# A new instruction order in the first pass and the first attention pairs of a two-layer decoder trunk

## The chip, the core and the metric

The kernel runs on one core of a Trainium2 chip, in one launch. The metric is device time in microseconds (us) of that launch. The kernel before took 774.13 us, the median of three runs (773.55 to 778.01).

## What is computed

The reference is a decoder trunk of two layers over 256 tokens of width 1024, all float32. A conditioning vector c gives each layer six modulation vectors by one large product, `silu(c) @ w_ada`. Each layer has a token mixer and a gated convolutional feed-forward block, each ahead of it normalised and modulated:

```python
for i in range(2):
    mod = jax.nn.silu(c) @ w_ada[i] + b_ada[i]
    sh1, sc1, g1, sh2, sc2, g2 = jnp.split(mod, 6, axis=-1)
    h = rmsnorm(x, norm_mix[i]) * (1 + sc1) + sh1
    y = dilated_mixture(h, ...) if i == 0 else gla_mixer(h, ...)
    x = x + g1 * y
    h = rmsnorm(x, norm_ffn[i]) * (1 + sc2) + sh2
    x = x + g2 * conv_ffn(h, ...)
return rmsnorm(x, norm_final)
```

The mixer of layer 0, the one that the change touches, has 16 heads of width 64 in three dilation groups. It needs `h @ w_in` for query, key and value of each group and head, scores with a relative bias, a softmax and the product with the values.

## The kernel before

**Arithmetic.** Activations lie transposed: 8 tiles `h[kt]` of 128 features by 256 tokens. A float32 product is made of three single-pass products: each weight tile and each activation tile is split into a rounded high part and a low part (the rest), and `mm3` (L172) issues high by high (L175), weights high by activation low (L176) and weights low by activation high (L177) into one PSUM bank. `split` (L155) loads a weight tile from memory into a buffer `raw`, ScalarE rounds it (`whi`, L165), VectorE subtracts (`wlo`, L169). There are four `raw` buffers, which the modulation weights share, and three each of `whi` and `wlo`. A buffer is handed on when its last reader is done.

**Queues.** All weight loads are issued in order by one queue, that of SyncE. Each compute engine executes its own instructions in order too. A planner that works with estimated durations orders the instructions of each engine at compile time; `with behind(i)` and `issue_after(i)` force what stands inside to come after instruction i on i's engine. PSUM has eight banks: two with the tag p, four with s, two with t. A new tile takes a bank of its tag when the tile that held it has been read for the last time.

**Start.** TensorE spreads c over the partitions (tile `cb`, L123), ScalarE applies silu (L124) into `c_bc`. The squares of x are summed (L357 to L363), TensorE adds them over the partitions (`ms`, L187), and ScalarE makes the reciprocal root (L189, L191). `keep_warm` (L266) issues matmuls whose result nobody reads. Three small matmuls (L377) make the bias rows in PSUM banks with tags t, t and s, and ScalarE copies them out (L392).

**First pass (L381 to L394 and L563 to L572).** For each of the 8 feature tiles VectorE makes two dot products of modulation weights with `c_bc` (`ada_chunk`, L138), ScalarE adds the offsets (L146, L148), VectorE scales x (`xr`, L257), ScalarE shifts and rounds (`hhi`, L259), VectorE takes the rest (`hlo`, L260) and the low part of 1920 columns of weights in two halves of 960. With these TensorE makes the projections of heads pair 0 and pair 1: twelve query and key products of 256 columns and two value products of 384, three matmuls each. The banks are s, s, s, p, p for pair 0 and its values and s, t, t for pair 1.

**Pairs 1 to 7.** `values` makes the value projections from two loads of 768 KB, `queries` a group's query and key from one of 1 MB, `evacuate` copies them from PSUM, `scores` makes the scores, `probabilities` the softmax, `turn` transposes the probabilities on TensorE through banks with the tag t (the copies out of it alternate between ScalarE and VectorE, L464), and `outputs` (L467) multiplies by the values. After each `queries` follows a chunk of modulation weights (`next_ada`). `load_bias` (L337) issues eight small loads per pair. After the first pass come, in this order, the first half of pair 1's values, the scores of pair 0, the second half, the first group of pair 2, the scores of pair 1, and then a loop over pairs 2 to 7 (L600 to L628).

Of the kernel before, what the change touches and what calls it, by code (L numbers as in the profile page):

```python
# [18 lines left out]
P = 128  # L19
D = 1024  # L20
# [37 lines left out]
def trunk(ctx: ExitStack, tc: tile.TileContext, I, out):  # L58
# [59 lines left out]


    c_bc = const.tile([P, D], F32, name="c_bc")  # L120
    for n in range(2):
        ps = bank("cb", "t")
        last_c = mm(ps, ones_d[:1, :], c_row[:1, 512 * n : 512 * n + 512], start=True, stop=True)  # L123
        silu = nc.scalar.activation(c_bc[:, 512 * n : 512 * n + 512], ps, AF.Silu, scale=float(D))  # L124


    mod = {}

    def ada_chunk(l, n, dmas=1):
# [4 lines left out]
        for s in range(2):  # L134
            piece, kt = ADA_ORDER[2 * n + s]
            dot = tmp.tile([P, 1], F32, tag="dot", name="dot", bufs=4)
            w = raw[:, D * s : D * s + D]
            nc.vector.tensor_tensor_reduce(  # L138
                w, w, c_bc, op0=ALU.mult, op1=ALU.add, scale=1.0, scalar=0.0, accum_out=dot,
            )  # L140
# [103 lines left out]

    @contextmanager
    def behind(*those):

        with ExitStack() as st:
            for i in those:
                st.enter_context(tc.issue_after(i.ins))  # L250
            yield

    def normed(l, sub, r, kt):
# [10 lines left out]
        return h_hi[kt], h_lo[kt]  # L264

    def keep_warm(n):  # L266

        ps = bank("warm")
        for i in range(n):
            mm(ps[:, :P], ones_d, ones_d, start=True, stop=True)  # L270

# [78 lines left out]

    sq = wspl.tile([P, 2048], F32, tag="wlo", name="sq").rearrange("p (k t) -> p k t", k=KT)
    with behind(last_c):
        keep_warm(4)
    nc.vector.tensor_tensor(sq[:, 0:4, :], x_all[:, 0:4, :], x_all[:, 0:4, :], op=ALU.mult)  # L357
    with behind(silu):
        for i in (4, 6):
            last_sq = nc.scalar.activation(sq[:, i : i + 2, :], x_all[:, i : i + 2, :], AF.Square)  # L360
    for n in (0, 4):
        for m in (2, 1):
            last_add = nc.vector.tensor_tensor(sq[:, n : n + m, :], sq[:, n : n + m, :], sq[:, n + m : n + 2 * m, :], op=ALU.add)  # L363
        if n == 0:
            with behind(last_add):
                last_add = scale_terms(0)
    exp_ln_after(last_sq)
# [11 lines left out]
    first = norm_ops[1], last_add  # L379
    w0, h = [], []  # L380
    for kt in range(KT):  # L381
        with behind(*first):
            term = ada_chunk(0, kt, dmas=1 if kt else 2)
        h.append(normed(0, 0, r, kt))
        if kt:
            w0.append(split(I["w0"][kt], 15 * P))
        else:
            with behind(chain[0][1]):
                w0.append(split(I["w0"][kt], 15 * P, 2, after=((term,), (chain[0][0],))))
            with behind(copied[0]):  # L390
                for ps, c in rows_ps:
                    nc.scalar.copy(rows[:, c], ps)  # L392
            first = (last_lo[0],)
        if kt == 1:  # L394
            scale_terms(1)
    with tc.issue_after(last_load[0].ins):
# [30 lines left out]

    def probabilities(s, bias):


        m = tmp.tile([P, 16], F32, tag="m", name="m")
        normed_p = []
        prob = [att.tile([P, KEYS + 2], F32, tag="prob", name="prob", bufs=6) for _ in range(4)]
        for i in range(4):
# [5 lines left out]
                op0=ALU.add, op1=ALU.max, scale=1.0, scalar=-3e38, accum_out=m[:, i : i + 1],  # L440
            )
        for h in range(2):
            rs, n = slice(2 * h, 2 * h + 2), KEYS + 2 * h
# [41 lines left out]

    last_q = [None]

    def evacuate(q, k, g, pq, pk):

        if g:
            last_q[0] = nc.scalar.mul(q[g], pq, 0.125)
            return nc.vector.tensor_copy(k[g], pk)
        qh, ql = q[0]
        nc.scalar.mul(qh, pq, 0.125)
        nc.vector.scalar_tensor_tensor(ql, pq, 0.125, qh.bitcast(F32), op0=ALU.mult, op1=ALU.subtract)
        pk = in_order(pk)
        kh, kl = (as_tokens(z[:, 0:T]) for z in k[0])
        nc.scalar.copy(kh, pk)  # L500
        return nc.vector.tensor_tensor(kl, pk, kh.bitcast(F32), op=ALU.subtract)

# [19 lines left out]

    def values(u, half, pv):
        with behind(*chain[7]):
            w = split(I["wv"][u - 1, half], 1536)
        for k4 in range(4):
# [6 lines left out]

    def queries(u, g, q, k, tag="p", after=()):
        w = split(I["wqk"][u - 2, g], 2048, after=(after, after))
        pqk = bank("pqk", tag)
        pq, pk = pqk[:, :T], pqk[:, T:]
        for kt in range(KT):
# [5 lines left out]
        with behind(evacuate(q, k, g, pq, pk)):  # L544
            next_ada()
        return middle, end

# [9 lines left out]

    b0 = [bank("pqk", tg) for tg in "ssspp"]
    pqk0 = [b[:, T * i : T * i + T] for b in b0[:3] for i in range(2)]
    pv = b0[3:]  # L560
    b1 = [bank("pqk", tg) for tg in "stt"]
    pqk1 = [b[:, T * i : T * i + T] for b in b1 for i in range(2)]
    for kt in range(KT):  # L563
        s, e = kt == 0, kt == KT - 1
        for i in range(2 * NG):
            mm3(pqk0[i], parts(w0[kt], P * i), h[kt], s and i % 2 == 0, e and i % 2 == 1)
        wv = parts(w0[kt], 6 * P, NG * P)
        for t in range(2):
            ht = [y[:, P * t : P * t + P] for y in h[kt]]
            mm3(pv[t][:, : NG * P], ht, wv, s, e)  # L570
        for i in range(2 * NG):
            mm3(pqk1[i], parts(w0[kt], 9 * P + P * i), h[kt], s and i % 2 == 0, e and i % 2 == 1)  # L572

    qk0, qk1 = new_qk(), new_qk()
    v = by_groups(pv)
    for qk, pqk, g in ((qk0, pqk0, 0), (qk1, pqk1, 0), (qk0, pqk0, 1), (qk0, pqk0, 2), (qk1, pqk1, 1), (qk1, pqk1, 2)):
        evacuate(*qk, g, pqk[2 * g], pqk[2 * g + 1])
    pv = [bank("pv", "p") for _ in range(2)]
    end = values(1, 0, pv)
    bias = bias_of(0)  # L580
    with behind(end):
        s, last = scores(*qk0)
    with behind(last):
        values(1, 1, pv)
    v0, v = v, by_groups(pv)
    before = probabilities(s, bias)

    qk = new_qk()
    with behind(last):
        end = queries(2, 0, *qk, tag="t", after=last_q)  # L590
    bias = bias_of(1)
    with behind(end[1]):
        turn((0, 1), *before)
        s, last = scores(*qk1)
    with behind(last):
        turn((2, 3), *before)
        outputs(0, v0, before[1])
    before = probabilities(s, bias)

    for u in range(2, NPAIR):  # L600
        if u > 2:
            bias = bias_of(u)
            qk = new_qk()
            with behind(last):
                queries(u, 0, *qk)
        middle, end = queries(u, 1, *qk)
        if u == 2:
# [5 lines left out]
        with behind(end):  # L613
            turned = turn((2, 3), *before)
        queries(u, 2, *qk)
        pv = [bank("pv", "p") for _ in range(2)]
        end = values(u, 0, pv)
        if u < NPAIR - 1:
            end = values(u, 1, pv)
# [7 lines left out]
        v = by_groups(pv)  # L627
        before = probabilities(s, bias)  # L628

# [543 lines left out]
```

## Time and profile before

| | |
|---|---|
| runs | 773.55, 774.13, 778.01 us; median 774.13 us |
| the profiled execution | 777.02 us, of which 775.1 us from the first to the last instruction (the span) |
| TensorE (PE) busy | 755.9 us, 98% of the span |
| VectorE (DVE) busy | 633.7 us, 82% |
| ScalarE (ACT) busy | 484.7 us, 63% |
| mean granted TensorE clock | 0.994 |
| DMA | 186.29 MB, mean 240 GB/s |

A busy TensorE is not one at its peak, since the ends of matmuls are modelled; the distance from one matmul's start to the next says more. Idle time of TensorE and stretches at a lower granted clock are what a new order could remove. The first 60 us are the start and the first pass, the stretch from there to about 275 us the attention pairs, and then come the output projection and the second half of layer 0, and layer 1.

### The profile page before, as it was taken

The page shows a single profiled execution, that of the slowest core. Times are in us where ns is not written, and L with a number is a line of the kernel's source. Part 1 is how long each engine was busy: PE and PEld are TensorE (multiplying, and loading weights), DVE is VectorE, ACT ScalarE, POOL GpSimd, SP SyncE. Part 2 cuts the span into 40 slices and gives each one's busy share as a digit, 9 for nine tenths or more (in the row PEclk, how much of TensorE's full clock was granted, in tenths as well). Part 3 has the DMA queues.
Part 4 walks back from the last instruction along what each step waited for, and adds up shares of the span by engine and source line. Part 5 has one row for each costly group of instructions (what it writes and reads, how often), then busy time and mean ns, then how long its engine had stood idle before and what let it go on. Part 6 is the DMA issues. An engine that isn't in the chain of part 4 may idle for free.

```text
span 775.1 us, 15908 instructions
## 1 busy us (share of the span) xinstructions
PE 755.9 (98%) x6416; PEld 731.5 (94%) x6416; DVE 633.7 (82%) x1136; ACT 484.7 (63%) x948; POOL 12.4 (2%) x36
## 2 busy tenths in 40 slices
PE   8899899999999999999999999999999999999997
PEld 5899899999999999999999998898999999999997
DVE  6996787779879968999998877797667998899662
ACT  5566564655666668766666556746667776667552
POOL 0000000000000010000000100000010000000000
PEclk9999999999999999999999999999999999999999
DMA  8988687686887847767646985966245665555741
GB/s 344 413 296 315 186 315 242 231 327 198 319 313 257 296 163 261 272 224 270 209 160 213 353 297 180 344 243 235 95 166 188 219 218 187 194 199 205 252 161 55
DMA packets 36199, 186.29 MB, mean 240 GB/s; under 512 B 8412, under 2 KB 10972, under 8 KB 19870
## 3 DMA queue, kind: packets, MB, share of 16 engines
q1 hardware_dynamic: 35744, 184.84, 66.8%
q8 instruction: 50, 0.82, 0.4%
q10 hardware_dynamic: 382, 0.45, 0.2%
q14 instruction: 23, 0.19, 0.1%
HBM read 184.17 MB, written 1.10 MB: 239 GB/s over the span
## 4 chain that ended last, share of the span: by engine, by line
PE 71%; DMA 12%; DVE 11%; ACT 3%; issue 1%; SPq 0%; DVEq 0%; ACTq 0%
PE pab L176 10%; PE pab L175 10%; PE pab L177 10%; DMA raw<-in_wqk 8%; DVE wlo L169 5%; PE pd L175 5%; PE pd L177 5%; PE pd L176 5%; DMA raw<-in_wv 3%; PE pqk L175 3%; PE pqk L176 2%; DVE ada_raw L138 2%; PE pqk L177 2%; PE py L175 2%; PE py L176 2%; PE py L177 2%
## 5 line engine op out<-in xcount | busy, mean ns | idle before, releaser
L169 DVE TENSOR_TENSOR wlo<-raw,whi 128x1024 fp32r<-128x1024 f32 (+3 forms) x274 | 291.8, 1098 | 62.8 <-ACT whi L165 62.1
L165 ACT CAST whi<-raw 128x1024 fp32r<-128x1024 f32 (+3 forms) x274 | 245.8, 945 | 131.9 <-PE pab L176 41.3
L177 PE MATMUL pab<-hhi,wlo 128*128 128x256 f32 x672 | 184.9, 276 | 0.0
L176 PE MATMUL pab<-hlo,whi 128*128 128x256 f32 x672 | 184.8, 277 | 0.0
L175 PE MATMUL pab<-hhi,whi 128*128 128x256 f32 x672 | 183.4, 277 | 0.0
L176 PEld LDWEIGHTS pab<-hlo,whi 128*128 128x128 f32 x672 | 126.1, 188 | 0.2
L177 PEld LDWEIGHTS pab<-hhi,wlo 128*128 128x128 f32 x672 | 126.2, 188 | 0.0
L175 PEld LDWEIGHTS pab<-hhi,whi 128*128 128x128 f32 x672 | 125.2, 188 | 0.1
L175 PE MATMUL pqk<-hhi,whi 128*128 128x256 f32 x440 | 120.8, 286 | 2.6 <-ACT hhi L259 2.6
L177 PE MATMUL pqk<-hhi,wlo 128*128 128x256 f32 x440 | 121.7, 281 | 0.0
L176 PE MATMUL pqk<-hlo,whi 128*128 128x256 f32 x440 | 121.6, 280 | 0.0
L138 DVE CUSTOM_DVE_ANT_0 ada_raw<-ada_raw,c_bc 128x1024 f32<-128x1024 f32 x96 | 113.6, 1222 | 6.6 <-DMA ada_raw<-in_w_ada 6.6
L177 PE MATMUL pd<-ghi,wlo 128*128 128x256 f32 x352 | 97.1, 276 | 0.0
L176 PE MATMUL pd<-glo,whi 128*128 128x256 f32 x352 | 97.1, 276 | 0.0
L175 PE MATMUL pd<-ghi,whi 128*128 128x256 f32 x352 | 96.8, 276 | 0.0
L175 PEld LDWEIGHTS pqk<-hhi,whi 128*128 128x128 f32 x440 | 82.3, 191 | 3.8 <-ACT hhi L259 3.1
L177 PEld LDWEIGHTS pqk<-hhi,wlo 128*128 128x128 f32 x440 | 83.4, 190 | 0.3 <-issue 0.3
L176 PEld LDWEIGHTS pqk<-hlo,whi 128*128 128x128 f32 x440 | 83.5, 190 | 0.1
L176 PEld LDWEIGHTS pd<-glo,whi 128*128 128x128 f32 x352 | 66.1, 188 | 0.0
L177 PEld LDWEIGHTS pd<-ghi,wlo 128*128 128x128 f32 x352 | 66.1, 188 | 0.0
L175 PEld LDWEIGHTS pd<-ghi,whi 128*128 128x128 f32 x352 | 65.9, 188 | 0.0
L734 ACT ACTIVATE r<-pab,small 128x256 f32<-128x256 f32 x86 | 46.6, 558 | 15.6 <-DVE r L737 15.5
(210 smaller groups left out, 1266.4 us busy)
## 6 DMA issues: line engine op xcount, KB each, us to landing
ada_raw<-in_w_ada SPq DMA_DIRECT2D x47, 1024.0 KB, 5.8
raw<-in_w_up SPq DMA_DIRECT2D x42, 1024.0 KB, 4.9
raw<-in_w_down SPq DMA_DIRECT2D x32, 704.0 KB, 5.1
raw<-in_wqk SPq DMA_DIRECT2D x18, 1024.0 KB, 6.6
raw<-in_wv SPq DMA_DIRECT2D x14, 768.0 KB, 4.6
raw<-in_w SPq DMA_DIRECT2D x7, 960.0 KB, 6.5
raw<-in_w_out_a SPq DMA_DIRECT2D x4, 1024.0 KB, 7.2
raw<-in_w_v_b SPq DMA_DIRECT2D x4, 1024.0 KB, 6.4
```

Source lines behind the costliest of these rows:

```text
L138: nc.vector.tensor_tensor_reduce(w, w, c_bc, op0=ALU.mult, op1=ALU.add, scale=1.0, scalar=0.0, accum_out=dot,)
L165: copied[0] = nc.scalar.copy(hi[:, c], raw[:, c])
L169: last_lo[0] = nc.vector.tensor_tensor(lo[:, c], raw[:, c], hi[:, c].bitcast(F32), op=ALU.subtract)
L175: mm(ps, a[0], b[0], start=start, stop=False)
L176: mm(ps, a[0], b[1], start=False, stop=False)
L177: return mm(ps, a[1], b[0], start=False, stop=stop)
L734: nc.scalar.activation(r, u[:, :T], AF.Identity, scale=cw[2], bias=col(C_CB + 44 * l + f))
```

## The change

- **Start.** Four `keep_warm` matmuls go to the head of TensorE's queue, ahead of the spreading of c. The two Squares on ScalarE go between the two silus. The second `keep_warm`, five matmuls, comes behind the bias rows, and the projections come behind it.
- **First pass on VectorE and ScalarE.** The order is written out by hand. Per tile: the two dot products, the first part of the low weights of the tile before (768 columns), `xr`, the second part (1152 columns), `hlo`; on ScalarE the offsets, `hhi`, and then both parts of `whi`. Tiles 0 and 1 have an order of their own. The copies of the bias rows come behind the `hhi` of tile 1.
- **First pass on TensorE.** The three products go by parts: high by high for a whole tile, then activation low, then weights low, the last of these interleaved with the next tile's. The banks are s, t, t, p, p and s, s, s.
- **Behind the pass.** Pair 2's first group comes first, by parts, then the scores of pair 0, both halves of pair 1's values, the scores of pair 1. The softmax is cut into `maxima` and `probabilities`. The outputs of pair 0 and the transposes of pair 1 move into the loop's turn for pair 2.
- **Transposes.** They use two t and two s banks, and ScalarE makes all copies.

```diff
+    keep_warm(4)
     c_bc = const.tile([P, D], F32, name="c_bc")
 ...
+        with behind(*((last_sq,) if n else ())):
+            silu = nc.scalar.activation(c_bc[:, 512 * n : 512 * n + 512], ps, AF.Silu, scale=float(D))
+        if n == 0:
+            with behind(silu):
+                for i in (4, 6):
+                    last_sq = nc.scalar.activation(sq[:, i : i + 2, :], x_all[:, i : i + 2, :], AF.Square)
 ...
     with behind(norm_ops[0]):
-        keep_warm(3)
 ...
-            mm(ps, tab[:, 16 * g : 16 * g + 16], oh[:33, c], start=True, stop=True)
+            last_row = mm(ps, tab[:, 16 * g : 16 * g + 16], oh[:33, c], start=True, stop=True)
             at += n
+    with behind(last_row):
+        warm = keep_warm(5)
 ...
+    dots(0)
+    scaled(0)
+    cast(0, 0)
+    shifted(0)
+    cast(0, 1)
+    rest_of(0)
+    low(0, 0)
+    dots(1)
+    low(0, 1)
+    scaled(1)
+    shifted(1)
+    rest_of(1)
+    with behind(on_act[0]):
+        for ps, c in rows_ps:
+            on_act[0] = nc.scalar.copy(rows[:, c], ps)
+    for kt in range(2, KT):
+        for half in range(2):
+            cast(kt - 1, half)
+        dots(kt)
+        low(kt - 1, 0)
+        scaled(kt)
+        low(kt - 1, 1)
+        shifted(kt)
+        rest_of(kt)
 ...
-            t = bank("t", "t")
+            t = bank("t", "ttss"[i])
 ...
-            (nc.vector.tensor_copy if i % 2 else nc.scalar.copy)(pt[:, i, :], t[:, 0:KEYS])
+            nc.scalar.copy(pt[:, i, :], t[:, 0:KEYS])
 ...
-    b0 = [bank("pqk", tg) for tg in "ssspp"]
+    b0 = [bank("pqk", tg) for tg in "sttpp"]
 ...
-    b1 = [bank("pqk", tg) for tg in "stt"]
+    b1 = [bank("pqk", tg) for tg in "sss"]
+    last = [warm]
+    def products(kt, part, pieces):
+        w, y = w0[kt][part == 2], h[kt][part == 1]
+        with behind(*last):
 ...
+        last[0] = i
     for kt in range(KT):
 ...
+        if kt:
+            products(kt - 1, 2, (0,))
+        products(kt, 0, range(3))
+        if kt:
+            products(kt - 1, 2, (1, 2))
+        products(kt, 1, range(3))
+    products(KT - 1, 2, (0,))
+    products(KT - 1, 2, (1, 2))
 ...
+    pq, pk, middle, end = raw_queries(2, 0, tag="t", low=left[2][1:], by_parts=True)
 ...
     with behind(end):
         s, last = scores(*qk0)
 ...
     with behind(last):
+        values(1, 0, pv, low=left[-1][1:])
+    end = values(1, 1, pv, after=left[-1][:1], low=evacuated[1:])
 ...
+    with behind(end):
         s, last = scores(*qk1)
+    raised = maxima(s, bias1)
 ...
+        if u == 2:
+            turned_pt, before = before[1], probabilities(*raised)
+        middle, end = queries(u, 2, *qk)
+        if u == 2:
+            with behind(end):
+                outputs(0, v0, turned_pt)
+                turn((0, 1), *before)
```

In the helpers `dots`, `scaled`, `shifted`, `rest_of`, `cast` and `low` each instruction stands behind the one that the order names before it on its engine (`on_dve`, `on_act`). `cast` and `low` work on columns 0 to 767 (the projections of pair 0) and 768 to 1919. The loads of tiles 0 and 1 go in two pieces.

## Rows read from the trace of the kernel before

**Rows 1.** The page's first section: busy time, share of the span, instructions of each engine.
```profile
PE 755.9 (98%) x6416; PEld 731.5 (94%) x6416; DVE 633.7 (82%) x1136; ACT 484.7 (63%) x948; POOL 12.4 (2%) x36
```

**Rows 2.** TensorE's waits, whole span: waiter, releaser, us in total, times, longest.
```profile
PE t L463 <- ACT pt L464: 4.3, 4, 2.6
...
PE pqk L175 <- ACT hhi L259: 2.6, 2, 2.2
...
PE po L471 <- DVE pt L464: 0.9, 1, 0.9
PE pv L175 <- DVE k L494: 0.8, 1, 0.8
PE s L418 <- DVE k L501: 0.8, 1, 0.8
```

**Rows 3.** Timeline of TensorE: start, duration, instruction, count, [idle before, releaser].
```profile
6.74 2.07 PE L270 MATMUL warm<-ones_d 128*128 128x128 f32 x8
...
11.87 1.47 PE L377 MATMUL rows<-oh,tab 33*16 33x512 f32 x6
13.72 0.62 PE L175 MATMUL pqk<-hhi,whi 128*128 128x256 f32 x3 [0.38 <-ACT hhi L259]
...
21.74 1.01 PE L175 MATMUL pqk<-hhi,whi 128*128 128x256 f32 x3 [2.25 <-ACT hhi L259]
...
28.63 0.52 PE L175 MATMUL pqk<-hhi,whi 128*128 128x256 f32 x3
...
33.84 0.52 PE L175 MATMUL pqk<-hhi,whi 128*128 128x256 f32 x3
...
59.87 0.34 PE L175 MATMUL pv<-whi,hhi 128*128 128x384 f32 x1
```

**Rows 4.** Two stretches of 3 us: busy per engine (instructions), granted clock, DMA share, GB/s.
```profile
22.00:25.00 3.00, 3.00 (x13) 3.00 (x14) 3.00 (x7) 2.32 (x4) 0.00 (x0) 0.50 1.02 417
83.50:86.50 3.00, 3.00 (x15) 3.00 (x16) 3.00 (x11) 0.37 (x1) 0.00 (x0) 0.50 0.96 401
```

**Rows 5.** Timeline of VectorE in the first pass.
```profile
9.58 1.22 DVE L138 CUSTOM_DVE_ANT_0 ada_raw<-ada_raw,c_bc 128x1024 f32<-128x1024 f32 x1
...
12.41 0.48 DVE L257 SCALAR_TENSOR_TENSOR xr<-x_all,mod,rstd 128x256 f32<-128x256 f32 x1 [0.46 <-ACT mod L146]
...
16.24 1.22 DVE L138 CUSTOM_DVE_ANT_0 ada_raw<-ada_raw,c_bc 128x1024 f32<-128x1024 f32 x1
...
18.53 2.22 DVE L169 TENSOR_TENSOR wlo<-raw,whi 128x960 fp32r<-128x960 f32 x2
...
23.35 0.48 DVE L260 SCALAR_TENSOR_TENSOR hlo<-xr,mod,hhi 128x256 fp32r<-128x256 f32 x1
...
28.57 0.48 DVE L260 SCALAR_TENSOR_TENSOR hlo<-xr,mod,hhi 128x256 fp32r<-128x256 f32 x1
```

**Rows 6.** Timeline of ScalarE in the first pass.
```profile
6.84 0.60 ACT L124 ACTIVATE c_bc<-cb 128x512 f32<-128x512 f32 x1 [1.11 <-PE cb L123]
7.34 1.14 ACT L360 ACTIVATE sq<-x_all 128x512 f32<-128x512 f32 x2
...
13.16 0.50 ACT L259 ACTIVATE hhi<-xr,mod 128x256 fp32r<-128x256 f32 x1
...
14.45 0.88 ACT L392 COPY rows<-rows 16x512 f32<-16x512 f32 x3
...
49.18 1.90 ACT L165 CAST whi<-raw 128x960 fp32r<-128x960 f32 x2 [0.45 <-DMA raw<-in_w]
```

**Rows 7.** The copies of the bias rows (L392): who waited for them (us, times).
```profile
  PEld pqk L175: 0.2, 1
```

**Rows 8.** Timeline of ScalarE around 82 us.
```profile
80.62 1.99 ACT L165 CAST whi<-raw 128x1024 fp32r<-128x1024 f32 x2 [3.11 <-DMA raw<-in_wqk]
...
82.92 0.47 ACT L464 COPY pt<-t 128x384 f32<-128x384 f32 x1
```

**Rows 9.** Timeline of TensorE: the transposes at 83 us.
```profile
83.45 0.90 PE L463 MATMUL t<-ident,pn 128*128 128x128 f32 x3 [2.65 <-ACT pt L464]
```

**Rows 10.** The chain that ended last: start us, us, what.
```profile
66.86 13.68 DMA raw<-in_wqk
...
251.20 0.45 PE pv L175
```

More of the change, by code (lines that the diff above doesn't have):

```diff
@@ L117, in scale_terms, with behind, keep_warm @@
                                               op0=ALU.add, op1=ALU.mult)
+    @contextmanager
+    def behind(*those):
+        with ExitStack() as st:
+            for i in those:
+                st.enter_context(tc.issue_after(i.ins))
+            yield
+    def keep_warm(n):
+        ps = bank("warm")
+        for i in range(n):
+            i = mm(ps[:, :P], ones_d, ones_d, start=True, stop=True)
+        return i
+    keep_warm(4)
     c_bc = const.tile([P, D], F32, name="c_bc")
+    sq = wspl.tile([P, 2048], F32, tag="wlo", name="sq").rearrange("p (k t) -> p k t", k=KT)
     for n in range(2):
@@ L123, in trunk @@
         last_c = mm(ps, ones_d[:1, :], c_row[:1, 512 * n : 512 * n + 512], start=True, stop=True)
-        silu = nc.scalar.activation(c_bc[:, 512 * n : 512 * n + 512], ps, AF.Silu, scale=float(D))
-    mod = {}
+        with behind(*((last_sq,) if n else ())):
[4 more added lines that the diff above has]
+                    last_sq = nc.scalar.activation(sq[:, i : i + 2, :], x_all[:, i : i + 2, :], AF.Square)
+    mod, last_dot = {}, [None]
     def ada_chunk(l, n, dmas=1):
@@ L243, in trunk @@
     squared = [None, None]
[L245 to L251, printed above, removed]
     def normed(l, sub, r, kt):
@@ L264, in normed @@
         return h_hi[kt], h_lo[kt]
[L266 to L270, printed above, removed]
     early_x = [state.tile([P, T + 16], F32, tag=f"ex{k}", name="early_x") for k in range(KT)]
@@ L351, in load_bias @@
         return both
-    sq = wspl.tile([P, 2048], F32, tag="wlo", name="sq").rearrange("p (k t) -> p k t", k=KT)
-    with behind(last_c):
-        keep_warm(4)
     nc.vector.tensor_tensor(sq[:, 0:4, :], x_all[:, 0:4, :], x_all[:, 0:4, :], op=ALU.mult)
-    with behind(silu):
-        for i in (4, 6):
-            last_sq = nc.scalar.activation(sq[:, i : i + 2, :], x_all[:, i : i + 2, :], AF.Square)
     for n in (0, 4):
@@ L363, in trunk @@
             last_add = nc.vector.tensor_tensor(sq[:, n : n + m, :], sq[:, n : n + m, :], sq[:, n + m : n + 2 * m, :], op=ALU.add)
[L364 to L367, printed above, removed]
+    with behind(last_add):
+        on_dve = [scale_terms(0)]
+    exp_ln_after(silu)
     r = rstd_of([sq[:, 0, :], sq[:, 4, :]])
@@ L376, in trunk @@
             rows_ps.append((ps, c))
-            mm(ps, tab[:, 16 * g : 16 * g + 16], oh[:33, c], start=True, stop=True)
+            last_row = mm(ps, tab[:, 16 * g : 16 * g + 16], oh[:33, c], start=True, stop=True)
             at += n
[L379 to L395, printed above, removed]
+    with behind(last_row):
+        warm = keep_warm(5)
@@ new lines, in trunk, with dots @@
+    w0, h, xr, raw0 = [], [], [None] * KT, []
+    pieces = (slice(0, 6 * P), slice(6 * P, 15 * P))
+    on_act = [norm_ops[1]]
+    def dots(kt):
+        with behind(on_dve[0], on_act[0]):
+            on_act[0] = ada_chunk(0, kt, dmas=2 if kt < 2 else 1)
+        on_dve[0] = last_dot[0]
+        raw = wraw.tile([P, 2048], F32, tag="raw", name="raw")
+        for c in pieces if kt < 2 else (slice(0, 15 * P),):
+            last_load[0] = nc.sync.dma_start(raw[:, c], I["w0"][kt][:, c])
+        raw0.append(raw)
+        w0.append([wspl.tile([P, 2048], F32R, tag=f"w{part}", name=f"w{part}") for part in ("hi", "lo")])
@@ new lines, in scaled, with shifted, rest_of @@
+    def scaled(kt):
+        xr[kt] = tmp.tile([P, T], F32, tag="xr", name="xr")
+        with behind(on_dve[0]):
+            on_dve[0] = nc.vector.scalar_tensor_tensor(xr[kt], x[kt], mod[0, 1, kt][:, 0:1], r, op0=ALU.mult, op1=ALU.mult)
+    def shifted(kt):
+        with behind(on_act[0]):
+            on_act[0] = nc.scalar.activation(h_hi[kt][:, :], xr[kt], AF.Identity, bias=mod[0, 0, kt][:, 0:1])
+    def rest_of(kt):
+        with behind(on_dve[0]):
+            on_dve[0] = nc.vector.scalar_tensor_tensor(h_lo[kt][:, :], xr[kt], mod[0, 0, kt][:, 0:1], h_hi[kt][:, :].bitcast(F32),
+                                                       op0=ALU.add, op1=ALU.subtract)
+        chain[kt] = chain[7] = on_act[0], on_dve[0]
+        h.append((h_hi[kt], h_lo[kt]))
@@ new lines, in cast, with low @@
+    def cast(kt, half):
+        c = pieces[half]
+        with behind(on_act[0]):
+            on_act[0] = nc.scalar.copy(w0[kt][0][:, c], raw0[kt][:, c])
+    def low(kt, half):
+        c = pieces[half]
+        with behind(on_dve[0]):
+            on_dve[0] = nc.vector.tensor_tensor(w0[kt][1][:, c], raw0[kt][:, c], w0[kt][0][:, c].bitcast(F32), op=ALU.subtract)
+    dots(0)
[7 more added lines that the diff above has]
+    low(0, 1)
@@ new lines, in trunk @@
+    scaled(1)
+    shifted(1)
+    rest_of(1)
+    with behind(on_act[0]):
+        for ps, c in rows_ps:
[9 more added lines that the diff above has]
+        rest_of(kt)
+    for half in range(2):
+        cast(KT - 1, half)
+    for half in range(2):
+        low(KT - 1, half)
+    scale_terms(1)
@@ L426, in scores, with maxima @@
         return s, last
-    def probabilities(s, bias):
+    def maxima(s, bias):
         m = tmp.tile([P, 16], F32, tag="m", name="m")
-        normed_p = []
         prob = [att.tile([P, KEYS + 2], F32, tag="prob", name="prob", bufs=6) for _ in range(4)]
@@ L441, in probabilities @@
             )
+        return prob, m
+    def probabilities(prob, m):
+        normed_p = []
         for h in range(2):
@@ L521, in new_qk, with values @@
         return q, k
-    def values(u, half, pv):
+    def values(u, half, pv, after=(), low=()):
         with behind(*chain[7]):
-            w = split(I["wv"][u - 1, half], 1536)
+            w = split(I["wv"][u - 1, half], 1536, after=(after, after), low=low, late=low)
         for k4 in range(4):
@@ L532, in values, with queries, raw_queries @@
         return end
-    def queries(u, g, q, k, tag="p", after=()):
-        w = split(I["wqk"][u - 2, g], 2048, after=(after, after))
+    def queries(u, g, *qk):
+        pq, pk, middle, end = raw_queries(u, g)
+        with behind(evacuate(*qk, g, pq, pk)[1]):
+            next_ada()
+        return middle, end
+    def raw_queries(u, g, tag="p", low=(), by_parts=False):
+        w = split(I["wqk"][u - 2, g], 2048, low=low, late=low)
         pqk = bank("pqk", tag)
         pq, pk = pqk[:, :T], pqk[:, T:]
+        if by_parts:
+            for part in range(3):
+                for kt in range(KT):
+                    for i, ps in enumerate((pq, pk)):
+                        at = 2 * P * kt + P * i
+                        end = mm(ps, w[part == 2][:, at : at + P], h[kt][part == 1], start=(part == kt == i == 0),
+                                 stop=(part == 2 and kt == KT - 1 and i == 1))
+            return pq, pk, None, end
         for kt in range(KT):
@@ L543, in queries @@
                 middle = end
-        with behind(evacuate(q, k, g, pq, pk)):
-            next_ada()
-        return middle, end
+        return pq, pk, middle, end
     def by_groups(pv):
@@ L574, in trunk @@
-    qk0, qk1 = new_qk(), new_qk()
[L575 to L579, printed above, removed]
+    last = [warm]
+    def products(kt, part, pieces):
+        w, y = w0[kt][part == 2], h[kt][part == 1]
+        s, e = part == kt == 0, part == 2 and kt == KT - 1
+        with behind(*last):
+            for piece in pieces:
+                if piece == 1:
+                    for t in range(2):
+                        i = mm(pv[t][:, : NG * P], y[:, P * t : P * t + P], w[:, 6 * P : 9 * P], start=s, stop=e)
+                    continue
+                at, ps = ((0, pqk0), None, (9 * P, pqk1))[piece]
+                for j in ((2, 3, 4, 5, 0, 1), (), range(6))[piece]:
+                    i = mm(ps[j], w[:, at + P * j : at + P * j + P], y, start=s and j % 2 == 0, stop=e and j % 2 == 1)
+        last[0] = i
@@ new lines, in trunk @@
+    for kt in range(KT):
+        if kt:
[6 more added lines that the diff above has]
+    products(KT - 1, 2, (1, 2))
+    qk0, qk1 = new_qk(), new_qk()
+    left = [evacuate(*qk, g, pqk[2 * g], pqk[2 * g + 1])
+            for qk, pqk, g in ((qk0, pqk0, 1), (qk0, pqk0, 2), (qk0, pqk0, 0), (qk1, pqk1, 0), (qk1, pqk1, 1), (qk1, pqk1, 2))]
+    pq, pk, middle, end = raw_queries(2, 0, tag="t", low=left[2][1:], by_parts=True)
@@ L580, in trunk @@
+    with behind(left[-1][0], left[-3][0]):
+        v0 = by_groups(pv)
     bias = bias_of(0)
@@ L582, in trunk @@
         s, last = scores(*qk0)
+    qk = new_qk()
+    evacuated = evacuate(*qk, 0, pq, pk)
+    pv = [bank("pv", "p") for _ in range(2)]
     with behind(last):
[L584 to L593, printed above, removed]
+        values(1, 0, pv, low=left[-1][1:])
+    end = values(1, 1, pv, after=left[-1][:1], low=evacuated[1:])
+    with behind(evacuated[1]):
+        next_ada()
+    v = by_groups(pv)
+    before = probabilities(*maxima(s, bias))
+    bias1 = bias_of(1)
+    with behind(end):
         s, last = scores(*qk1)
[L595 to L598, printed above, removed]
+    raised = maxima(s, bias1)
     for u in range(2, NPAIR):
@@ L603, in trunk @@
             qk = new_qk()
-            with behind(last):
+        with behind(last):
+            if u > 2:
                 queries(u, 0, *qk)
-        middle, end = queries(u, 1, *qk)
+            middle, end = queries(u, 1, *qk)
         if u == 2:
@@ L614, in trunk @@
             turned = turn((2, 3), *before)
-        queries(u, 2, *qk)
+        if u == 2:
[5 more added lines that the diff above has]
+                turn((0, 1), *before)
         pv = [bank("pv", "p") for _ in range(2)]
         end = values(u, 0, pv)
+        if u == 2:
+            with behind(end):
+                turned = turn((2, 3), *before)
         if u < NPAIR - 1:
@@ L627, in trunk @@
         v = by_groups(pv)
-        before = probabilities(s, bias)
+        before = probabilities(*maxima(s, bias))
     def between(n, kt):
```

24 lines of the change are left out of this document (7 added, 17 removed).

## The prediction

> **What bounds the kernel now.** I read the page first. TensorE is busy for 98% of the span [rows 1], so a new order can give back no more than its idle time, its stretches at the lower clock and what the start costs. Next, TensorE's waits [rows 2]: few, and the largest that the change touches are 2.6 us for a transpose and 2.2 us for the second tile of the first pass. Third, TensorE's timeline [rows 3]: tiles 2 and 3 begin 5.21 us apart (28.63 and 33.84) and no wait ends there, so this is TensorE's own pace for one tile; tile 1, begun at 21.74 after the idle 2.25 us, takes 6.89 us. The stretch view says why: after that idle the granted clock is 0.50, which is 1.2 of 2.4 GHz, and after the wait at 83.45 it is so again [rows 4, 9]. VectorE needs 5.22 us for a tile (23.35 to 28.57 [rows 5]). So inside the pass the two engines are level, and the order on VectorE is worth something only where TensorE actually waits for it: at the head.
>
> **The start.** The Squares (1.14 us) began right behind the second silu, begun at 6.84 [rows 6]; now they stand ahead of it. The trace does not show when the second half of x arrives, only that it is there at 7.34. The dot products, begun at 9.58 [rows 5], start 0 to 1.6 us sooner; I take 0.8, the middle, so 8.8. The early warm matmuls run while TensorE has nothing else to do, and cost nothing.
>
> **The head of the pass: the step that decides.** The bias rows are computed into both t banks and one s bank. Before, the products' first banks were s, s, s, p, p, and ScalarE copied the rows out at 14.45 [rows 6]; even so a weight load waited 0.2 us for those copies [rows 7]. Now the five warm matmuls take the next bank in turn, a t; the first products want both t banks; every product stands behind the warm ones; and the copies stand on ScalarE behind tile 1's `hhi`. So TensorE's first product waits for tile 1's `hhi`, which hangs on a long VectorE chain. From 8.8: two dots 2.3 (16.24 to 18.53 [rows 5]), so 11.1; `xr` starts 11.6 (before, 2.8 us after the first dot); `hhi` starts 0.75 later and takes 0.5 [rows 5, 6], so 12.8; `hlo` 0.4, 13.2; low part of 768 columns 0.9 (2.22 us per 1920 [rows 5]), 14.1; dots of tile 1, 16.4; low part of 1152 columns 1.3, 17.7; `xr` 0.4 and `hhi` 0.5, 18.6; first copy (of 0.88 us for three [rows 6]), about 19.1. Five warm matmuls at the low clock take about 2.3 us (four took 2.07 [rows 3]). The first product then starts near 21.4 instead of 13.72 [rows 3].
>
> From there TensorE has eight tiles of 5.21 us, 41.7 us. It had been idle since the bias rows, so it restarts at the low clock; the warm matmuls pay part of that. Tile 1 of before lost 1.7 us so; I take 0.7, between 0 and 1.7, because two of the three microseconds lie under the warm matmuls. The end of the pass is 21.4 + 41.7 + 0.7 = 63.8 against 59.87 [rows 3]: **+3.9 us**. VectorE does not hold it up: from 19 it needs six more tiles and a last low part, 19 + 6 × 5.22 + 2.3 = 53, and the last weights, which came at 49.18 [rows 6], come at about the same time, both well before TensorE reaches tile 7 near 58. That cover of 5 us also pays for the `raw` buffers: a tile's weights are now freed one pair of dots later.
>
> The Trainium skill (TensorE: Matmul & The Clock Gate, the section on HAM oscillation) says that a burst of matmuls after a long wait starts cold every time; the trace agrees, 0.50 after 2.25 us of idle. By that rule alone, with nothing paid by the warm matmuls, the pass would end 1.0 us later than I take.
>
> **Behind the pass.** Pair 2's first weights, now first in line, are in long before. By parts, their low half is wanted two thirds of the way through, 3.8 us in, and VectorE has by then only three evacuations of 0.4 us and the low part itself. Then scores of pair 0: their 0.8 us wait for `k` [rows 2] goes, since 5.6 us of products lie between: **-0.8**. The wait of 2.65 us at 83.45 was for a t bank whose copy stood on ScalarE behind a rounding that waited for its load until 80.62 and ran 1.99 us [rows 8, 9]. With four banks, four transposes need no copy in between: **-2.6**, and the 3 us at half clock behind it [rows 4] give **-1.5**. Of the later waits (t banks 4.3 - 2.6 = 1.7, `po` 0.9, `pv` 0.8 [rows 2]) four banks can take the first, but ScalarE has two copies of 0.47 us more per pair [rows 8] and VectorE two fewer; bounds 0 and 3.4, I take **-1.7**. What is late next is the third load of pair 2.
>
> **Sum.** 3.9 - 0.8 - 2.6 - 1.5 - 1.7 = -2.7. The profiled execution took 777.02 us, 2.9 above the median of 774.13; the sum is made in its span and set against the median: 771.4. Within this mechanism it runs from 768.5 (start 1.6 earlier, all later waits gone) to 775.5 (clock loss whole, later waits stay). Later stages see no edit but the earlier date.
>
> **Rivals.**
> - *The bank does not hold the products* (the planner finds the warm matmuls and the first products another bank, or puts the copies sooner). Then tile 0 starts near 12.8, runs 34 of its 42 matmuls and stops for tile 1's `whi`, cast behind the copies at about 20.2. From there 37.5 us of work are left: end 57.7, or 59.4 with the clock loss. That is -0.5 to -2.2 in place of +3.9, so 765.3 to 767. For it: the pass was written to start early. Against: [rows 7] shows that products do wait for these copies, and nothing in the order lets the copies go before.
> - *The load wait comes back: slower.* Pair 2's third load gets its buffer when pair 1's second low part is done, some 9 us behind the pass, near 73. Before, that load took 13.68 us [rows 10], with three others ahead of it. TensorE wants it at 63.8 + 5.6 + 2 + 8.4 + 2 + 5.6 + 1.4 = 88.8 (48 products of 256 columns, scores, 48 of 384, scores, 48 of 256, twelve transposes). 73 + 13.7 + 2 for rounding and low part is 88.7. If it lands later than that, TensorE stands still again, goes to the low clock again, and the 4.1 us of the second and third gain are lost with the 1.7: 774.1 + 3.9 - 0.8 = 777.2. For it: all copies now stand on ScalarE, the engine that waits for loads [rows 8]. Against: the load's queue is shorter, since pair 2's first weights have already gone.
>  The Trainium skill (PSUM — Partial Sum Buffer, section on engine and sequencer instructions) calls ScalarE's queue strictly first in, first out; the trace agrees: the copy at 82.92 ran only behind the rounding that waited 3.11 us.
> - *The loading chain keeps its dates: no change.* From the load at 66.86 to the product at 251.20 the chain of waits [rows 10] goes through loads, rounding and low parts, and TensorE is 0.8 us behind it at the end [rows 2]. If nothing in that chain moves, whatever TensorE gains before 251 is lost there: 774. Against: one load has been moved ahead of it, and VectorE has two copies per pair fewer.
>
> **Chances.** My forecast 0.45, the early start 0.17, the load wait 0.18, the unmoved chain 0.20. Faster by over 1% (what can be told from no change in this kernel) means under 766.4: half of the early start and a little of the forecast, 0.11. Slower by over 1% is above 781.9: only the load wait with more than one such stop, 0.04. Within 1%: 0.85. The range takes in the forecast's bounds, the unmoved chain, the load wait at 777.2 and most of the early start: 765 to 778. The forecast's own range is 768.5 to 775.5.
>
> **What would show it.** In the profile after: the first product behind the copies of the bias rows, at 20 to 22 us, with idle TensorE ahead of it and the clock at 0.50; the next phase beginning at 63 to 65; no wait at L463; no stop of 2 us or more between 65 and 110. A first product at about 13 us makes the step on the bank wrong, and the time falls under 768. A TensorE wait for `whi` or `wlo` of pair 2's third group makes the load wait right. A longer wait at the end of the pairs, near 250, is the unmoved chain.

## The result and the profile after

The changed kernel takes 777.5 us (median of 22 runs, 775.35 to 781.55) against 775.08 us for the kernel before beside it (22 runs, 772.85 to 778.03): ratio 1.0033, 95% interval 1.002 to 1.0047. Another set of 12 runs gave 779.33 against 774.75, ratio 1.0043 (1.0023 to 1.0064). The change costs 0.3 to 0.4%; the forecast was a gain of 0.35%.

The page's first section [rows 1]:
```profile
PE 757.8 (98%) x6420; PEld 731.9 (94%) x6420; DVE 625.5 (80%) x1120; ACT 490.7 (63%) x964; POOL 12.4 (2%) x36
```
VectorE has 8.2 us less to do, ScalarE 6.0 us more: the copies of the transposed probabilities (`pt`) have moved from one to the other, 16 instructions.

TensorE's waits [rows 2]; columns as there:
```profile
PE warm L132 <- ACT rows L433: 6.4, 1, 6.4
PE pv L197 <- DVE k L547: 1.4, 1, 1.4
PE po L526 <- ACT pt L519: 1.3, 1, 1.3
...
PE t L518 <- ACT pt L519: 0.4, 1, 0.4
...
PE s L470 <- ACT pt L519: 0.2, 1, 0.2
```
The waits of the transposes (`t`) have shrunk from 4.3 to 0.4 us, and the one of the first scores for `k` (0.8) is gone. New ones stand in their place, for the same copies (`pt`): by `po`, the product of the probabilities with the values, and by the scores `s`. The wait of the value products (`pv`) for `k` has grown from 0.8 to 1.4 us. Ahead of them all stands the bias rows' wait.

TensorE's timeline [rows 3, 9]:
```profile
19.12 2.50 PE L132 MATMUL warm<-ones_d 128*128 128x128 f32 x10 [6.38 <-ACT rows L433]
21.27 0.77 PE L641 MATMUL pqk<-hhi,whi 128*128 128x256 f32 x2
...
22.45 1.10 PE L641 MATMUL pqk<-hhi,whi 128*128 128x256 f32 x8
...
64.16 2.05 PE L602 MATMUL pqk<-hhi,whi 128*128 128x256 f32 x16
...
96.52 1.08 PE L526 MATMUL po<-pt,v 128*64 128x256 f32 x8 [1.29 <-ACT pt L519]
...
108.41 0.62 PE L470 MATMUL s<-k,q 64*128 64x258 f32 x3 [0.24 <-ACT pt L519]
```
The first product comes at 21.27, not 13.72; the pass ends at 64.16 (first product of the next phase), not 59.87.

VectorE's first dot product [rows 5], and ScalarE's copies of the bias rows [rows 6, 7]:
```profile
8.79 1.22 DVE L160 CUSTOM_DVE_ANT_0 ada_raw<-ada_raw,c_bc 128x1024 f32<-128x1024 f32 x1
```
```profile
18.51 0.87 ACT L433 COPY rows<-rows 16x512 f32<-16x512 f32 x3
```
The dots start 0.79 us sooner; the copies run 4 us later than before, and what waits for them is no longer 0.2 us of a weight load but TensorE itself.

Stretches [rows 4]:
```profile
21.30:22.40 1.10, 1.10 (x6) 1.10 (x6) 1.10 (x3) 0.45 (x2) 0.00 (x0) 1.00 0.98 410
22.40:25.40 3.00, 3.00 (x26) 3.00 (x26) 3.00 (x5) 2.29 (x3) 0.00 (x0) 1.00 1.01 404
83.50:86.50 3.00, 3.00 (x28) 3.00 (x28) 3.00 (x10) 2.21 (x6) 0.00 (x0) 1.00 0.35 58
534.40:537.80 3.40, 3.40 (x19) 3.40 (x18) 3.40 (x4) 2.20 (x3) 0.00 (x0) 0.50 0.82 289
```
Both stretches at the low clock have gone. (In this profile the granted clock reads 1.00 at the first product too, while the matmuls there still run at about half their later pace: two of 256 columns take 0.58 us from 21.27, eight take 0.93 us from 22.45.) One is new at 534, in layer 1, behind a wait of 0.9 us for `wlo` that the kernel before has too, at the same place and without a loss of clock.

ScalarE [rows 8] and the chain [rows 10]:
```profile
94.52 1.56 ACT L187 CAST whi<-raw 128x768 fp32r<-128x768 f32 x2 [1.32 <-DMA raw<-in_wv]
96.00 0.47 ACT L519 COPY pt<-t 128x384 f32<-128x384 f32 x1
```
```profile
86.57 7.93 DMA raw<-in_wv
...
95.21 5.33 DMA raw<-in_wqk
```
As before at 80.62, a copy stands on ScalarE behind a rounding that waits for its load (7.93 us from 86.57); now `po` waits for it.

### The profile page after: what moved, and what is told of

The parts are those of the page before. It is cut to its first block, busy times and chain, and to the rows that moved or that the text cites. A ratio compares the mean times of both kernels' runs of the same rounds, so it can differ in the third digit from the quotient of the medians.

```text
span 777.1 us, 15925 instructions
## 1 busy us (share of the span) xinstructions
PE 757.8 (98%) x6420; PEld 731.9 (94%) x6420; DVE 625.5 (80%) x1120; ACT 490.7 (63%) x964; POOL 12.4 (2%) x36
## 4 chain that ended last, share of the span: by engine, by line
PE 71%; DMA 13%; DVE 11%; ACT 3%; issue 2%; SPq 0%; DVEq 0%; ACTq 0%
PE pab L199 10%; PE pab L198 10%; PE pab L197 10%; DMA raw<-in_wqk 7%; PE pd L197 5%; PE pd L199 5%; PE pd L198 5%; DVE wlo L191 5%; PE pqk L641 4%; DMA raw<-in_wv 4%; DVE ada_raw L160 2%; PE py L197 2%; PE py L198 2%; PE py L199 2%; ACT whi L187 2%
## 5 line engine op out<-in xcount | busy, mean ns | idle before, releaser
L191 DVE TENSOR_TENSOR wlo<-raw,whi 128x1024 fp32r<-128x1024 f32 (+2 forms) x258 | 273.7, 1094 | 56.6 <-ACT whi L187 55.9
L187 ACT CAST whi<-raw 128x1024 fp32r<-128x1024 f32 (+2 forms) x258 | 230.5, 942 | 115.8 <-PE pab L198 40.7
L197 PE MATMUL pqk<-hhi,whi 128*128 128x256 f32 x328 | 92.4, 282 | 0.0
L199 PE MATMUL pqk<-hhi,wlo 128*128 128x256 f32 x328 | 91.3, 279 | 0.0
L198 PE MATMUL pqk<-hlo,whi 128*128 128x256 f32 x328 | 91.1, 278 | 0.0
L197 PEld LDWEIGHTS pqk<-hhi,whi 128*128 128x128 f32 x328 | 61.8, 188 | 0.5
L199 PEld LDWEIGHTS pqk<-hhi,wlo 128*128 128x128 f32 x328 | 61.7, 188 | 0.3 <-issue 0.3
L198 PEld LDWEIGHTS pqk<-hlo,whi 128*128 128x128 f32 x328 | 61.7, 188 | 0.0
```

The source lines that it names most:

```text
L187: copied[0] = nc.scalar.copy(hi[:, c], raw[:, c])
L191: last_lo[0] = nc.vector.tensor_tensor(lo[:, c], raw[:, c], hi[:, c].bitcast(F32), op=ALU.subtract)
L197: mm(ps, a[0], b[0], start=start, stop=False)
L198: mm(ps, a[0], b[1], start=False, stop=False)
L199: return mm(ps, a[1], b[0], start=False, stop=stop)
```

## Experiments

Theory A: TensorE sets the pace of the pairs, so the late first product is paid in full. Theory B, the rival of the unmoved chain: loads keep the dates up to 250 us. Theory C, added later: the removed stop came back at other instructions. Each time is a median, its ratio one to the kernel before, run beside it, with a 95% interval. Edits are shown shortened; square brackets stand for lines left out. Dates from a profile are those of one execution.

**e1_rows_early**
```
-    rest_of(1); [copies of the bias rows]
+    cast(0, 1); [copies of the bias rows]; rest_of(0)
-            ps = bank("rows", "tts"[i])
+            ps = bank("rows", "sss"[i])
```


> The three copies of the bias rows go ahead on ScalarE, behind the casts of tile 0, and the rows are computed in three s banks instead of two t and one s. Theory A (TensorE sets the pace of the attention pairs, so the late first product is paid in full): the first product starts at 13 to 15 us instead of 21.3, the first pass ends 4.5 to 6.5 us sooner than in the changed kernel, and so does the kernel: 771 to 773 against 777.5. Theory B (the chain of loads keeps its dates whatever TensorE does before 250 us): the pass ends just as much sooner, TensorE then waits for weights between 65 and 250, the last pair ends where it did, 776.5 to 778.

774.41 us (12 runs), ratio 0.9989 (0.9969 to 1.0009): 3 us below the change (777.5), short of 771 to 773. TensorE:
```profile
12.63 2.50 PE L132 MATMUL warm<-ones_d 128*128 128x128 f32 x10
14.78 1.02 PE L641 MATMUL pqk<-hhi,whi 128*128 128x256 f32 x4
...
58.64 2.05 PE L602 MATMUL pqk<-hhi,whi 128*128 128x256 f32 x16
```
The pass ends at 58.64, 5.5 us sooner. The second scores are still 5.5 us ahead, layer 0's first projection behind the pairs only 2.64: half was lost near 90 us, where `po` now waits 2.5 us for `pt` and the clock falls. Neither theory alone.

**e1a_copies_early**: the first of those two edits alone.

> The changed kernel with the copies of the bias rows behind tile 0's casts, in the banks they had (two t, one s). If the late copies held the bank, the warm matmuls begin behind them at 14.6 us, the first product at 17: 4.3 us sooner than 21.3, and the pass ends 3 to 5.5 us sooner, as with the s banks, since tile 1 is not there before 20: 773 to 775. If the banks themselves hold it: 777.5.

774.8 us (12 runs), ratio 0.9999 (0.9982 to 1.0017). The first product comes at 16.46, the pass ends at 59.86:
```profile
14.30 2.50 PE L132 MATMUL warm<-ones_d 128*128 128x128 f32 x10 [1.55 <-ACT rows L426]
16.46 0.77 PE L641 MATMUL pqk<-hhi,whi 128*128 128x256 f32 x2
...
59.86 2.05 PE L602 MATMUL pqk<-hhi,whi 128*128 128x256 f32 x16
```
The interval lies below that of the change (1.002 to 1.0047). So the order of three copies on ScalarE is the whole of the loss; with it right, the rest of the change is worth nothing that can be measured.

**e4_later_start**
```
-        warm = keep_warm(5)
+        warm = keep_warm(21)
```


> The changed kernel with 21 warm matmuls in place of 5 ahead of the first product. Sixteen more at 0.25 to 0.5 us put the first product 4 to 5 us later, with the products of tile 0 then all at the high clock (0.5 us back). Theory A: the end moves by as much, 781 to 782. Theory B: TensorE waits less for weights in the pairs, the last pair ends within 1 us of where it did, 777.5 to 778.5.

779.89 us (6 runs), ratio 1.0055 (1.0034 to 1.0076). The first product comes 4.94 us later (26.21), the pass ends 4.45 later (68.61), the pairs 4.22. Against Theory B: nothing takes the delay up, TensorE's waits in the pairs are 3.3 us, against 3.3 to 3.9 in the three executions of the change below. The median, between the two expectations, moved by 2.4 only (0.6 against the second set of runs of the change, 779.33), so it tells less than the profile.

**e2_four_banks_alone**
```
-            t = bank("t", "t")
+            t = bank("t", "ttss"[i])
```


> The kernel before, with four banks in place of two for the transposes and nothing else. Theory A: the wait of 2.65 us at 83 us and the half clock behind it go and stay gone, 4 us off 775.1: 771. Theory B: they go, but the last pair ends at the same date: 774.5 to 775.5.

776.81 us (12 runs), ratio 1.0014 (0.9997 to 1.0032). The wait did not go:
```profile
82.85 0.55 PE L463 MATMUL t<-ident,pn 128*128 128x128 f32 x3 [2.10 <-ACT pt L464]
```
The transpose waits for the copy out of the one before it, since in the old order pair 2's first products hold a t bank as well. Four banks alone do not remove the stop.

**e5_two_banks**: the reverse edit in the changed kernel.

> The changed kernel with two banks for the transposes, as before the change; all copies stay on ScalarE. Theory A (TensorE sets the pace, every wait of TensorE in the pairs is paid at the end): each transpose pair waits for a copy behind a rounding, 2 to 5 us of new waits and half clock: 779 to 783 against 777.5. Theory B (loads keep the dates): 777.5.

780.75 us (6 runs), ratio 1.0077 (1.0052 to 1.0101). TensorE's waits from 60 to 260 us:
```profile
PE t L518 <- ACT pt L519: 3.6, 5, 1.6
PE po L526 <- ACT pt L519: 1.3, 1, 1.3
```
In the new order the transposes wait 3.6 us for copies with two banks and 0.4 with four. The median is 1.4 to 3.3 us higher (against 779.33 and 777.5), but the intervals of the sets overlap, so what four banks are worth in time is not settled.

**e3_copies_alternate**
```
-            nc.scalar.copy(pt[:, i, :], t[:, 0:KEYS])
+            (nc.vector.tensor_copy if i % 2 else nc.scalar.copy)(pt[:, i, :], t[:, 0:KEYS])
```


> The changed kernel with the copies of the transposes alternating between ScalarE and VectorE again, four banks kept. Theory A: the wait of 1.3 us of po for the copies at 96.5 goes, 776.2 against 777.5. Theory B: 777.5, no move at the last pair.

783.73 us (6 runs), ratio 1.01 (1.0075 to 1.0126): slower than the change, against the expectation. The wait of `po` goes, but:
```profile
PE pv L197 <- DVE k L547: 3.3, 2, 2.0
PE s L470 <- ACT pt L519: 2.2, 1, 2.2
```
```profile
110.00:113.00 3.00, 3.00 (x47) 2.12 (x47) 2.29 (x11) 1.62 (x3) 0.20 (x2) 0.50 0.86 276
```
The scores wait for a copy on ScalarE, the clock falls (second fence), and `k` comes later from VectorE, which has two copies per pair back. Taking copies off VectorE was worth having: 4.4 to 6.2 us.

**e8_again, e12_after_third, e11_before_again**: both kernels unchanged.

> The changed kernel once more. If the half clock at 534 us (1.5 us in the gate of layer 1, behind a wait of 0.9 us that both kernels have) belongs to the change, its profile shows it again. If not, it is the chance of one execution, and the span from the gate's first product to the end is 238 us as in the other kernels, not 239.7. Time 777.5 in either case.

> The changed kernel a third time, for its profile: first product at 21.3, pass ended at 64, po or s waiting 1 us for the copies near 96; a half clock may stand at one of the three waits of about 1 us, or at none.

> The kernel before once more, for its profile. Its profiled execution of 777.0 lies 1.9 above its median; if that is one late transfer or one half clock, this one lacks it and ends near 775. The waits in the pairs (2.65 at 83 and the half clock behind it) stand in both.

779.33 us (12 runs; the profiled execution 775.66); 781.41; 772.65. Dates in us, from the timelines:

| execution | pass ends | second scores end | pairs end (first `py`) | last matmul ends |
|---|---|---|---|---|
| before | 59.87 | 78.95 | 260.76 | 770.10 |
| before, again | 58.60 | 77.70 | 256.41 | 765.72 |
| after | 64.16 | 81.58 | 260.68 | 772.14 |
| after, again | 64.31 | 81.73 | 259.72 | 768.91 |
| after, third | 65.35 | 82.77 | 264.30 | 774.64 |

The third execution of the change has no low clock at 534 but one at 110, behind the scores' wait for `pt`; the second has neither. The scores in the second, then TensorE, ScalarE and the stretch in the third:
```profile
108.42 0.62 PE L470 MATMUL s<-k,q 64*128 64x258 f32 x3 [1.06 <-ACT pt L519]
```
```profile
110.50 1.01 PE L470 MATMUL s<-k,q 64*128 64x258 f32 x3 [2.10 <-ACT pt L519]
```
```profile
107.70 1.99 ACT L187 CAST whi<-raw 128x1024 fp32r<-128x1024 f32 x2 [3.64 <-DMA raw<-in_wqk]
109.60 0.85 ACT L519 COPY pt<-t 128x384 f32<-128x384 f32 x2
```
```profile
110.60:117.00 6.40, 6.40 (x67) 5.17 (x68) 5.13 (x14) 5.81 (x16) 0.20 (x2) 0.50 0.56 189
```
This is what Theory C says: two of the four transposes stand in s banks, the next scores want those banks, and the copies out of them stand behind a rounding that waits for its load. In the three executions that wait is 0.24, 1.06 and 2.10 us.

**e13_copies_first**
```
-        w = split(I["wqk"][u - 2, g], 2048, low=low, late=low)
+        w = split(I["wqk"][u - 2, g], 2048, low=low, late=low,
+                  after=(last_pt if u > 2 and g == 0 else (), ()))
```


> The changed kernel with the rounding of each later pair's first group (from pair 3) put behind the copies of the transposes on ScalarE. Two of the four transposes now use s banks, and in the three profiles of the changed kernel the scores of pair 2 wait 0.24, 1.06 and 2.10 us for their copies, which stand behind a rounding that waits for its load; one of the three times with 6.8 us at half clock behind it. Theory C (the removed wait of the transposes came back there): the wait goes, 1.1 us and a third of 3.4 us on average: 775 to 776.5 against 777.5 and 779.3. If those waits only show a load that TensorE waits for anyway, its products wait next: no difference.

In its profile (776.5 us) the waits of `po` and of the scores are gone; the pairs end at 258.56, 1.2 to 5.7 us sooner than in the three above. But the median of 6 runs is 779.35, ratio 1.0058 (1.0037 to 1.0079). Where the wait comes from is shown; that its removal shortens the kernel is not.

**e6_bias_later**: e1_rows_early, and
```
-        if u == 2: bias = bias_of(u); [reload of x]
+        if u == 2: [reload of x]
             ...
             end = values(u, 1, pv)
+        if u == 2: bias = bias_of(u)
```


> The kernel with the early bias rows (774.4), and the eight transfers of pair 2's bias issued behind the two loads of its value weights instead of ahead of them. If the wait of 2.5 us of po and the half clock behind it come from those loads, issued only at 82.8 behind the transfers and awaited by the rounding at 87.4 that the copies stand behind: the loads go out near 72, po does not wait, 4 us off: 770.5. If the copies are late for another reason (VectorE's pn, the order on ScalarE): 774 to 775.

770.94 us (12 runs), ratio 0.9955 (0.993 to 0.9979): faster than both kernels, as expected. SP's queue, first with the early rows alone, then with this edit:
```profile
78.59 0.45 SPq L352 DMA_DIRECT2D bias<-rows_d  x1
82.13 0.60 SPq L353 DMA_DIRECT2D bias<-rows_d  x1
82.83 1.04 SPq L181 DMA_DIRECT2D raw<-in_wv  x2
```
```profile
74.86 8.09 SPq L181 DMA_DIRECT2D raw<-in_wv  x2
82.98 0.45 SPq L352 DMA_DIRECT2D bias<-rows_d  x1
```
The first of the two value loads goes out 8 us sooner; the `whi` rounding that the copies stand behind then starts at 82.88 instead of 87.42, and neither `po` nor the scores wait. TensorE from 80 to 110:
```profile
80.00:110.00 30.00, 29.70 (x286) 28.05 (x286) 22.58 (x51) 20.68 (x49) 0.19 (x2) 1.00 0.72 244
```
The whole early start arrives at the end of the pairs: against the first profile of the change the pass ends 5.5 us sooner, the pairs 6.08 (254.60).

**e10_bias_only**: the same move without the early rows.

> The changed kernel with pair 2's bias issued behind the loads of its value weights; the bias rows stay late. Theory A: the wait of po (1.3 us) goes, and the stretch from the second scores to the third shortens by up to what it did in the kernel with both edits (3.5 us in time): 774.5 to 776.5 against 777.5, and the two edits add up. If the wait only paid because the pass had ended early: 777.5.

780.5 us (6 runs), ratio 1.0058 (1.0041 to 1.0075): no faster than the change, against the expectation; the two edits do not add up. `po` no longer waits, but
```profile
90.67 0.88 PE L518 MATMUL t<-ident,pn 128*128 128x128 f32 x3 [2.20 <-DVE pn L508]
```
On VectorE a low part now stands ahead of the maxima, and so of `pn`, and waits for its rounding; the stop is back one step earlier.
```profile
85.61 1.23 DVE L191 TENSOR_TENSOR wlo<-raw,whi 128x1024 fp32r<-128x1024 f32 x1 [3.32 <-ACT whi L187]
```

**e7_bias_x_later**: e6_bias_later with the reload of x at `u == 4`.

> As the one with pair 2's bias later, and the reload of x (1 MB, wanted only behind the pairs) moved from pair 2 to pair 4. If the load of pair 2's second group (9.2 us from 69.33) is slow because x is in transfer beside it, it lands 2 to 3 us sooner and TensorE's wait of 1.9 us for k behind it shrinks: up to 2 us better than with the bias alone. If the buffers pace the loads: no difference.

774.54 us (12 runs), ratio 0.9991 (0.9971 to 1.0011): 3.6 us worse than without. The order on ScalarE changed with it, and a product waits for the values' copies, so the run says nothing on the load.
```profile
82.09 0.58 PE L197 MATMUL pqk<-hhi,whi 128*128 128x256 f32 x1 [4.11 <-ACT v L564]
```

**e14_all_three**: e6_bias_later and the edit of e13_copies_first.

> Early bias rows, pair 2's bias behind the value loads, and the rounding behind the copies. The profile of the first two edits together (770.9) has no wait of the scores, so the third adds little on the median: 769.5 to 771; its slow executions (up to 777) become rarer if they were that wait.

771.43 us (12 runs), ratio 0.9951 (0.9927 to 0.9974): level with e6_bias_later.

## Why the prediction was wrong

**The start was right**: dots 0.79 us sooner against 0.8. **The head was right, and a little dearer**: copies at 18.5 (forecast 19.1), first product 21.27 (21.4), pass ended at 64.16 (63.8), 4.3 us against 3.9. A tile took 5.29 us (31.36 to 36.65), not 5.21. By the second executions of both kernels the cost is 5.7, since the first pass before ended at 58.60 there. The step that I called decisive decided: e1a_copies_early moves three copies and the loss is gone.

**The failing step is "Behind the pass"**: -0.8, -2.6, -1.5 and -1.7, 6.6 us in all. By the table, from the end of the pass to the second scores the change gains 1.7 us: 1.3 at the first scores, where `k` was late, and 0.4 for one transposed tile (three matmuls) that now comes later. From there to the end of the pairs before took 181.81 and 178.71 us (mean 180.3), after 179.10, 177.99 and 181.53 (mean 179.5): 0.7 gained, 1.1 without that tile, where 5.8 was forecast; no pairing of these executions gives more than 3.8. In all that is 2.4 us regained in place of 6.6, against a head of 4.3 to 5.7: that is a loss of 1.9 to 3.3 us, and its medians lie 2.4 and 4.6 above the kernel before. The experiments say the same without the late head: with the pass ended at 58.64 and 59.86, e1_rows_early and e1a_copies_early should by this step have come to 766.3 and 767.5 (774.13 with their head and -6.6), and took 774.41 and 774.8. Three things made the difference.
- *The stop was read from one execution.* In the other one of before it is 1.91 us, and the later t waits 0.5 instead of 1.7:
```profile
81.45 0.80 PE L463 MATMUL t<-ident,pn 128*128 128x128 f32 x3 [1.91 <-ACT pt L464]
```
 The waits from the second scores on are 6.0 and 1.9 + 1.5 = 3.4 us in the two, so that less was there to be had than I summed. The profiled execution was 2.9 us over the median of the three runs that I had (1.9 over that of 22); I set the sum against the median but left its terms at that execution's size.
- *The reason for the wait stayed.* "Four transposes need no copy in between" holds but for 0.4 us in one of three executions. But two of the four banks are those of the scores, and ScalarE still copies behind roundings that wait for loads. `po` and the next scores wait in the transposes' stead, 1.1 to 2.1 us together, once with the clock behind it (e12_after_third). I asked what is late next and named a load, not who wants the lent banks back. This is read from the traces; e13_copies_first, which removes these waits, did not lower the median.
- *The later waits*, -1.7, hardly shrank. By execution 3.9, 3.3 and 3.8 us of waits remain between the second scores and the end of the pairs. Without those of `po` and the scores for `pt` that is 2.4, 2.2 and 1.7 us, where the two executions of before had 3.4 and 1.5 beside the stop.

The bounds of 768.5 and 775.5 do not follow from the terms that the prediction names for them: an earlier start (-0.8) and no later waits (-1.7) give 768.9, the whole clock loss (+1.0) and all later waits (+1.7) give 774.1.

**The rivals.** *The bank does not hold the products*: it holds the warm matmuls ahead of them, by 6.38 us. *The load wait comes back*, at 777.2, has the sign and nearly the time, 777.5: the mechanism (all copies on ScalarE behind roundings that wait) is the one found, but at `po` and the scores, while the third group's `whi` and `wlo`, where I priced it, do not stop TensorE. That the time agrees is luck: the rival has 3.9 for the head and regains 0.8, where 4.3 to 5.7 and 2.4 were measured. The Trainium skill's sentence on ScalarE's queue (PSUM — Partial Sum Buffer, section on engine and sequencer instructions: strictly first in, first out) is borne out once more by the copy at 109.60 behind the rounding at 107.70. *The loading chain keeps its dates* looks right in the first pair of profiles, with the pairs' ends at 260.76 and 260.68. It is wrong: e6_bias_later moves that date by -6.08, 5.1 us ahead of the earliest execution of the change, and the median with it. e4_later_start moves it by +4.22 (264.90), which alone would say little, since the third execution of the change ended the pairs at 264.30. The equal dates are a cost of 4.3 and a gain that happened to match it in those two executions.

**The clock.** The sign that I named, a granted clock of 0.50 at the first product, did not come: the profile reads 1.00 there. By the matmuls' starts the pace was half until 22.45, 1.2 us after the first product, and about 0.6 us was lost, near the 0.7 that I took. The stretch behind the stop at 83 did go, but in two of the three executions of the change one came elsewhere, at 534 and at 110.

**What stays open.** Why the median of e13_copies_first did not follow its profile, and how the runs of one kernel come to differ by 5 us, of which the executions here show waits of changing size and the clock behind them as a part.

## What to carry over

When banks, buffers or copies are moved to take a wait away, ask who else wants the lent bank and what stands ahead of the copy on its engine: if the copy still queues behind an instruction that waits for a load, the wait comes back under another name. Look at the order on a helper engine's queue at the head of a pass with the same care as at the work itself: three copies of 0.87 us in all, put behind one long chain, cost more (4.3 to 5.7) than the rest of the new order brought (2.4). And size the terms of a sum by more than one execution where they are waits of 1 to 3 us.

## What was not expected of the hardware

- Equal waits of TensorE are not equally dear. After 1.29 and 1.06 us of idle (changed kernel, near 96 and 108) the clock stayed high; after 2.10 us 6.4 us ran at 0.50, and after a wait of 0.9 us at 533, 3.4 us did so in one execution of the change and in neither of the others. In e4_later_start a wait of 1.33 us at 112 was enough.
- Transfers of 32 and 64 KB on SP's queue waited for 1 MB loads ahead of them, and held the loads behind them. With the early rows alone the eight transfers of a pair went out from 72.06 to 82.73 us; SP's waits from 60 to 100 us there:
```profile
SPq L353 <- DMA ada_raw<-in_w_ada: 5.8, 3, 3.1
```
